# The last gate of a decoder trunk: squares of two token blocks side by side, the last norm's vector on ScalarE, the third block ahead of the fourth, bias rows earlier

## The chip, the cores and the metric

The kernel runs on one core of a Trainium2 chip. The time is the device time of one execution in microseconds, as a median of runs. The core's engines are TensorE (PE: matmuls, PEld: its weight loads), VectorE (DVE), ScalarE (ACT), GpSimd (POOL) and SyncE (SP, which here only issues DMAs). Each engine works its own instruction queue in order, and engines wait for each other by semaphores. DMAs are issued from an engine's queue, here SP's and ScalarE's.

## The reference

A decoder trunk of two layers on 512 tokens of 1024 features, in float32. This is the part that bears on the change: the second layer's gated per-layer embedding and the final norm.

```python
def rmsnorm(x, g):
    xf = x.astype(jnp.float32)
    y = xf * lax.rsqrt(jnp.mean(xf * xf, axis=-1, keepdims=True) + EPS)
    return (y * g.astype(jnp.float32)).astype(x.dtype)

def per_layer_embed(h, p_i, g_norm, w_in, w_gate, b_gate):
    gate = jax.nn.sigmoid(rmsnorm(h, g_norm) @ w_gate + b_gate)
    return (p_i @ w_in) * gate

    for i in range(DEPTH):
        ...
        h = h + conv_ffn(rmsnorm(h, norm_ffn[i]), f_w_up[i], f_conv_w[i], f_conv_b[i], f_w_down[i])
        h = h + per_layer_embed(h, p[i], norm_ple[i], ple_w_in[i], ple_w_gate[i], ple_b_gate[i])
        ...
    return rmsnorm(h, norm_final)
```

## The kernel before

The residual `h` lies with features on the partitions: eight tiles of 128 features x 512 tokens. Every float32 matmul is made of three matmuls on operands that are split into a high and a low part (`mm3`, and `mm3t` where the result has tokens on the partitions; their matmuls have lines L190 to L192 and L201 to L203). Everything up to the last gate runs this way.

The last gate works with tokens on the partitions. There are four token blocks `i` of 128 tokens, and for each the 1024 features in two halves `n` of 512 (for the last block one half and two quarters of 256, see `cuts`). `gate_t(i, n)` issues the matmuls of one such part into a PSUM tile `gt`, 24 of them; the very last part starts with one more matmul, from `rows` (L986), which adds the bias inside the sum. `gated_t(i, n, ps)` issues what follows: `zt`, the scaling by the token's root mean square and the bias (VectorE, L999), the sigmoid `st` (ScalarE, L1004; L996 for the last part, straight from PSUM), the multiply by the embedding `pet` (VectorE, L1005), the add of the residual (VectorE, L1014 for blocks 0 and 1, in place in `hT`; L1021 into `hm` for blocks 2 and 3), and the sum of squares (ScalarE, L1015 and L1023; VectorE, L1028, in the last two parts). For blocks 2 and 3 the result is also multiplied by the last norm's vector `grow` (GpSimd, L1031; VectorE, L1035, into `yt` in the last block).

The residual has to come over to this layout. VectorE transposes it in squares of 32x32 (`turn`, L918: `turned_a` for tokens 0 to 255, `turned_b` for 256 to 511), and `places` (L929) then moves the rows of squares between partitions by DMAs within SBUF into `hT[0]` (blocks 0 and 1) and `hT[1]` (blocks 2 and 3), sixteen DMAs of 64 KB each from SP's queue.

`scaled(i)` makes the final norm's factor of a block: a sum (`fms`, L1040), scale and epsilon (`fin..m`, L360), the power -1/2 on GpSimd (`fin..rt`, L362), for blocks 0 and 1 the multiply by `grow` (VectorE, L1046), then the scaling by the factor (ScalarE, L1047), and for block 2 the DMA to the output. Blocks 0 and 1 are written with features on the partitions: `back()` moves the squares of `hT[0]` back (sixteen DMAs, eight from SP's queue and eight from ScalarE's), transposes them (VectorE, L1057, into `y`) and writes `y` out in four DMAs. `end()` scales the last block by its factor `rfin` (GpSimd, L1063; then ScalarE and VectorE, L1066 and L1068) and writes it.

`bias_rows()` makes the rows that the last part's extra matmul needs. It calls `npl.spread`, which makes `np1d` on VectorE (L342) and then a matmul `np1sp` on TensorE (L346); VectorE's reciprocal (L960) reads that, and a few small casts follow.

The calls stand in the order that is printed at the end of the function. From them a scheduler builds each engine's queue: TensorE's matmuls stay close to the order of the calls, and the other engines' instructions are placed among each other by it. `behind(ins, front)` adds an order of its own: the instruction `ins` stands behind `front` on the same engine. In the kernel before, TensorE's queue has in this stage: the first halves of blocks 0 and 1, the second halves of blocks 0 and 1, the spread `np1sp`, the first halves of blocks 2 and 3, the second half of block 2, and the two quarters of block 3.

Of the kernel before, what the change touches and what calls it, by code (L numbers as in the profile page):

```python
# [8 lines left out]
F32 = mybir.dt.float32  # L9
F32R = mybir.dt.float32r  # L10
AF = mybir.ActivationFunctionType
ALU = mybir.AluOpType

P = 128
D = 1024
S = 512
KD = D // P
# [5 lines left out]
N = S // 2  # L23
# [25 lines left out]
def tile_yoco(ctx: ExitStack, tc: tile.TileContext, t, out: bass.AP, out_b: bass.AP):  # L49
    nc = tc.nc  # L50
# [5 lines left out]
    wp = ctx.enter_context(tc.tile_pool(name="wp", bufs=1))  # L56
# [4 lines left out]
    def psum(name):  # L61
        return mmp.tile([P, S], F32, tag="mm", name=name)
# [60 lines left out]
    def behind(ins, front):  # L123

        tc.add_manual_dep(ins.ins, front.ins.name,
                          mybir.DependencyInfo(mybir.DependencyClass.NoSync, mybir.DependencyReason.DATA),
                          reason="order")
# [80 lines left out]
    def v(name, i):  # L208
        c = VEC[name] + i
        return vec[:, c : c + 1]  # L210

    h = [hp.tile([P, S], F32, tag=f"h{k}", name=f"h{k}") for k in range(KD)]
# [25 lines left out]
    ps = psum("idle").rearrange("p (a b) -> p a b", a=4)  # L238
# [37 lines left out]
    class Norm:  # L276
# [27 lines left out]
        def turn(self):  # L304

            sq = tp.tile([P, S], F32, tag="sq", name=f"{self.name}turn")
            nc.vector.transpose(sq, self.acc)
            self.quarter = const.tile([P, S // 32], F32, tag="quarter", bufs=1, name=f"{self.name}quarter")
            nc.vector.tensor_reduce(self.quarter, sq.rearrange("p (b f) -> p b f", f=32),
                                    axis=mybir.AxisListType.X, op=ALU.add)  # L310
# [265 lines left out]
    for c in range(4):  # L576
# [4 lines left out]
        for j in range(2):  # L581
            m = 2 * c + j
            ps = ups[j]
            z = tp.tile([P, S], F32, tag="hs", name=f"uz{m}")
            nc.vector.tensor_mul(z, ps, rstd)
            u = tp.tile([P, S], F32, tag="sg", name=f"u{m}")
# [20 lines left out]
    turned = const.tile([KD, 2, P], F32, name="turned")  # L607
    ps = psum("turned")
    for i, (name, l) in enumerate((("ple_b_gate", 1), ("norm_final", 0))):
        c0 = VEC[name] + l * KD  # L610
# [97 lines left out]
    box = {}  # L708
# [200 lines left out]
    SQ = 32  # L909
    NQ = P // SQ  # L910

    def squares(pool, tag, name):
        return pool.tile([P, N // SQ, KD, SQ], F32, tag=tag, bufs=1, name=name)

    turned_a = squares(at, "vtl", "turned_a")

    def turn(x, m, c):
        nc.vector.transpose(x[:, :, m, :], h[m][:, c * N : (c + 1) * N].rearrange("p (b t) -> p b t", t=SQ))  # L918

    npl.behind = lambda m: turn(turned_a, m, 0)  # L920
    pet = ffn(1, nf, npl)
# [1 line left out]
    def places(x, y, there):  # L923

        for b in range(NQ):
            for a in range(NQ):
                u = x[SQ * a : SQ * (a + 1), b::NQ].rearrange("p b m d -> p b (m d)")
                w = y[SQ * b : SQ * (b + 1), :, a, :]
                (nc.scalar if a % 2 and not there else nc.sync).dma_start(*((w, u) if there else (u, w)))  # L929


# [8 lines left out]
    parts2 = chunk(S, KD, ahead=2 * WBUFS)  # L940
    r = [f"r{(state['turn'] + j) % 3}" for j in range(3)]
    turned_b = squares(wp, r[0], "turned_b")
    hT = [wp.tile([P, 2, NQ, KD * SQ], F32, tag=r[1 + c], bufs=1, name=f"hT{c}") for c in range(2)]
    places(turned_a, hT[0], True)
    for m in range(KD):
        turn(turned_b, m, 1)
# [3 lines left out]
    brow, grow = (mp.tile([P, D], F32, tag=tag, name=f"row_{tag}") for tag in ("m4", "m5"))  # L950
# [8 lines left out]
    def bias_rows():  # L959
        nc.vector.reciprocal(whole_f[:, 3 * P :], npl.spread(S // 64 - 2, 2))  # L960
        for n, a, at0, lows in ((P, whole_f[:, 3 * P :], 0, 64), (2 * P, brow[:, D - 2 * P :], P, 32)):
            cols = slice(at0, at0 + n)
            nc.scalar.copy(whole[:, cols], a)
            for q in (0, 32, 64):
                if q == lows:
                    nc.vector.tensor_sub(rows[q : q + 1, cols], a[q : q + 1], whole_f[q : q + 1, cols])
                else:
                    nc.scalar.copy(rows[q : q + 1, cols], a[q : q + 1])
# [8 lines left out]
    def by_square(x):  # L977
        return x.rearrange("p (m a d) -> p a m d", a=NQ, d=SQ)

    def gate_t(i, n):  # L980

        c0, w = cuts[i][n]
        ps = psum(f"gt{i}_{n}")[:, :w]
        end = i == LAST and n == len(cuts[i]) - 1
        if end:
            nc.tensor.matmul(ps, rows[:, :P], rows[:, P : 3 * P], start=True, stop=False)  # L986
        mm3t(ps, xs, parts2 if c0 >= S else parts, c0 % S, w, i, first=not end)
        return ps

    def gated_t(i, n, ps):  # L990
        c0, w = cuts[i][n]
        end = i == LAST and n == len(cuts[i]) - 1
        r = rt[:, i : i + 1]
        sg = tp.tile([P, w], F32, tag="sg", name=f"st{i}_{n}")
        if end:
            nc.scalar.activation(sg, ps, AF.Sigmoid, scale=r)  # L996
        else:
            z = tp.tile([P, w], F32, tag="hs", name=f"zt{i}_{n}")
            ins = nc.vector.scalar_tensor_tensor(z, ps, r, brow[:, c0 : c0 + w], op0=ALU.mult, op1=ALU.add)  # L999
            if "y" in box:  # L1000
                behind(ins, box["y"])
            if (i, n) == (LAST, 1):
                behind(ins, box["hm"])
            nc.scalar.activation(sg, z, AF.Sigmoid)  # L1004
        ins = nc.vector.tensor_mul(sg, sg, pet[i][:, c0 : c0 + w])  # L1005
        if end:
            behind(ins, box["yt"])
        turned = hT[i // 2][:, i % 2, :, c0 // NQ : (c0 + w) // NQ]
        sq = tp.tile([P, w], F32, tag="sq", name=f"sqt{i}_{n}")
        if i < 2:  # L1010

            held[i, n] = turned
            split = turned.rearrange("p a (m d) -> p a m d", d=SQ)
            nc.vector.tensor_add(split, split, by_square(sg))  # L1014
            nc.scalar.activation(sq.rearrange("p (a f) -> p a f", a=NQ), turned, AF.Square,  # L1015
                                 accum_out=ssq[:, i, n : n + 1])
            return
        if c0 % S == 0:
            held[i, c0 // S] = tp.tile([P, S], F32, tag=("c0", "acc")[i % 2], name=f"hm{i}_{n}")
        hm = held[i, c0 // S][:, c0 % S : c0 % S + w]  # L1020
        box["hm"] = nc.vector.tensor_add(by_square(hm), turned.rearrange("p a (m d) -> p a m d", d=SQ), by_square(sg))  # L1021
        if i < LAST or n == 0:
            nc.scalar.activation(sq, hm, AF.Square, accum_out=ssq[:, i, n : n + 1])  # L1023
        else:

            if n == 1:
                nc.vector.tensor_scalar(total[:, :1], ssq[:, i, :1], 1.0 / D, EPS, op0=ALU.mult, op1=ALU.add)
            nc.vector.tensor_tensor_reduce(out=sq, in0=hm, in1=hm, scale=1.0 / D, scalar=total[:, n - 1 : n],  # L1028
                                           op0=ALU.mult, op1=ALU.add, accum_out=total[:, n : n + 1])
        if i < LAST:  # L1030
            nc.gpsimd.tensor_mul(hm, hm, grow[:, c0 : c0 + w])  # L1031
        else:
            if not yt:
                yt.append(mp.tile([P, D], F32, tag="m0", name="yt"))
            box["yt"] = nc.vector.tensor_mul(yt[0][:, c0 : c0 + w], hm, grow[:, c0 : c0 + w])  # L1035

    def scaled(i):

        ms = const.tile([P, 1], F32, tag="fms", bufs=2, name=f"fms{i}")
        nc.vector.tensor_reduce(ms, ssq[:, i], axis=mybir.AxisListType.X, op=ALU.add)  # L1040
        r = inv_root(ms, f"fin{i}", 1.0 / D)
        for n in range(2):
            hm = held[i, n]
            if i < 2:
                split = hm.rearrange("p a (m d) -> p a m d", d=SQ)
                nc.vector.tensor_mul(split, split, by_square(grow[:, n * S : (n + 1) * S]))  # L1046
            nc.scalar.activation(hm, hm, AF.Copy, scale=r[:, :1])  # L1047
            if i >= 2:
                nc.sync.dma_start(out_b[i - 2, :, n * S : (n + 1) * S], hm)

    def back():

        x = squares(at, "vtl", "turned_y")
        places(x, hT[0], False)
        y = wp.tile([P, KD, N], F32, tag=r[0], bufs=1, name="y")
        for m in range(KD):
            box["y"] = nc.vector.transpose(y[:, m, :].rearrange("p (b t) -> p b t", t=SQ), x[:, :, m, :])  # L1057
            if m % 2:
                nc.sync.dma_start(out[m - 1 : m + 1].rearrange("k p s -> p k s"), y[:, m - 1 : m + 1, :])

# [9 lines left out]

    for i in range(2):
        gated_t(i, 0, pss[i])
    for i in range(2):
        gated_t(i, 1, gate_t(i, 1))
        scaled(i)
    bias_rows()
    for i in (2, 3):
        gated_t(i, 0, gate_t(i, 0))
    back()
    gated_t(2, 1, gate_t(2, 1))  # L1080
    scaled(2)
    for n in (1, 2):
        gated_t(3, n, gate_t(3, n))
    end()


# [64 lines left out]
```

## Time and profile before

| what | us |
|---|---|
| median of 3 runs (lowest, highest) | 1133.78 (1132.97, 1133.96) |
| the profiled execution's own time | 1134.12 |
| its span, first to last instruction | 1132.4 |
| busy: TensorE, VectorE, ScalarE, GpSimd | 1120.2, 760.1, 513.2, 103.0 |
| mean granted TensorE clock | 0.998 |

A row of the profile in order of time gives the start and the duration in microseconds, the engine, the line of the kernel, the operation, the tile written and the tiles read (buffer numbers left out), the shapes, and how many instructions in a row it stands for; in brackets, the idle time of the engine before it and what ended it. A row of a group gives busy time in all and the mean of one in ns, then the idle time before the group. A row of a DMA tile gives the shortest, median and longest issue in ns. The rows called SPq and ACTq are DMA issues in the queues of SP and ScalarE. The last row of times by window has the window, its length, the busy time of PE, PEld, DVE, ACT and POOL (with instructions), the granted clock, the DMA share and GB/s.

### The profile page before, as it was taken

To read this page: it belongs to the slowest core of one execution; us is meant where nothing else is said; L and a number is where in the kernel's file an instruction comes from. 1 tells how busy PE (TensorE), PEld (TensorE's weight loads), DVE (VectorE), ACT (ScalarE), POOL (GpSimd) and SP (SyncE) were. 2 spreads that over 40 slices of the span, in tenths; PEclk is the share of its full clock that TensorE was granted. 3 is DMA by queue.
4 is the path that set the end of the run, shared out by engine and by line. 5 is a ranking of instruction groups with operands and counts; after the bars stand their busy time and mean duration, and the time that the engine had idled before them with its cause. 6 is when DMAs were issued, how large, how long until landed. Compare 5 with 4: busy or idle time off the path is not lost.

```text
span 1132.4 us, 13327 instructions
## 1 busy us (share of the span) xinstructions
PE 1120.2 (99%) x5118; PEld 930.3 (82%) x5118; DVE 760.1 (67%) x1178; ACT 513.2 (45%) x811; POOL 103.0 (9%) x163
## 2 busy tenths in 40 slices
PE   9999999999999999999999999999999999999996
PEld 7888888888888888888888888888888888888885
DVE  7366477763577457656988997777636773675786
ACT  6533454431334234544656775444313431344543
POOL 2000210000000000012204441000000000000211
PEclk9999999999999999999999999999999999999999
DMA  8322323232222322233134223323222223224333
GB/s 288 135 107 75 112 75 112 78 109 104 83 102 70 109 110 89 98 112 112 49 101 130 75 94 114 130 93 112 77 110 101 77 102 112 90 73 162 109 88 112
DMA packets 29472, 118.55 MB, mean 105 GB/s; under 512 B 3672, under 2 KB 11616, under 8 KB 19936
## 3 DMA queue, kind: packets, MB, share of 16 engines
q1 hardware_dynamic: 28352, 116.71, 30.3%
q10 hardware_dynamic: 1056, 0.98, 0.3%
q8 instruction: 40, 0.66, 0.2%
q14 instruction: 24, 0.20, 0.1%
HBM read 108.24 MB, written 2.11 MB: 97 GB/s over the span
## 4 chain that ended last, share of the span: by engine, by line
PE 92%; DVE 4%; ACT 1%; issue 1%; DMA 1%; POOL 0%; SPq 0%; POOLq 0%; DVEq 0%; ACTq 0%
PE up L190 14%; PE up L192 14%; PE up L191 14%; PE d L192 8%; PE d L190 8%; PE d L191 8%; PE gate L190 1%; PE gate L192 1%; PE u L191 1%; PE u L190 1%; PE u L192 1%; PE gate L191 1%; PE o L191 1%; PE o L192 1%; PE o L190 1%
## 5 line engine op out<-in xcount | busy, mean ns | idle before, releaser
L163 ACT CAST wh<-wraw 128x1024 fp32r<-128x1024 f32 (+2 forms) x197 | 202.1, 1028 | 265.0 <-PE d L191 131.3
L164 DVE TENSOR_TENSOR wl<-wraw,wh 128x1024 fp32r<-128x1024 f32 (+1 forms) x198 | 238.5, 1206 | 122.2 <-ACT wh L163 121.6
L190 PE MATMUL up<-nf00h,wh 128*128 128x512 f32 x352 | 137.1, 390 | 0.0
L190 PE MATMUL up<-nf10h,wh 128*128 128x512 f32 x352 | 137.0, 389 | 0.0
L192 PE MATMUL up<-nf00h,wl 128*128 128x512 f32 x352 | 137.0, 389 | 0.0
L192 PE MATMUL up<-nf10h,wl 128*128 128x512 f32 x352 | 137.0, 389 | 0.0
L191 PE MATMUL up<-nf10l,wh 128*128 128x512 f32 x352 | 137.0, 389 | 0.0
L191 PE MATMUL up<-nf00l,wh 128*128 128x512 f32 x352 | 137.0, 389 | 0.0
L190 PE MATMUL d<-ah,wh 128*128 128x512 f32 x352 | 136.9, 389 | 0.0
L191 PE MATMUL d<-al,wh 128*128 128x512 f32 x352 | 136.9, 389 | 0.0
L192 PE MATMUL d<-ah,wl 128*128 128x512 f32 x352 | 136.9, 389 | 0.0
L403 ACT ACTIVATE c<-hs,vec 128x512 f32<-128x512 f32 x88 | 71.5, 815 | 72.8 <-DVE hs L399 72.1
L404 DVE SCALAR_TENSOR_TENSOR c<-hs,vec,c 128x511 f32<-128x511 f32 x88 | 65.8, 748 | 34.2 <-ACT c L403 34.2
L379 DVE TENSOR_TENSOR h<-h,d 128x512 f32<-128x512 f32 x56 | 38.4, 686 | 72.7 <-PE d L192 72.7
L192 PEld LDWEIGHTS up<-nf10h,wl 128*128 128x128 f32 x352 | 66.1, 188 | 13.8
L191 PEld LDWEIGHTS up<-nf00l,wh 128*128 128x128 f32 x352 | 66.1, 188 | 13.8
L192 PEld LDWEIGHTS d<-ah,wl 128*128 128x128 f32 x352 | 66.1, 188 | 13.7
L191 PEld LDWEIGHTS d<-al,wh 128*128 128x128 f32 x352 | 66.1, 188 | 13.7
L190 PEld LDWEIGHTS up<-nf10h,wh 128*128 128x128 f32 x352 | 66.1, 188 | 13.7
L190 PEld LDWEIGHTS d<-ah,wh 128*128 128x128 f32 x352 | 66.1, 188 | 13.7
L192 PEld LDWEIGHTS up<-nf00h,wl 128*128 128x128 f32 x352 | 66.1, 188 | 13.7
L190 PEld LDWEIGHTS up<-nf00h,wh 128*128 128x128 f32 x352 | 66.1, 188 | 13.6
(406 smaller groups left out, 1953.4 us busy)
## 6 DMA issues: line engine op xcount, KB each, us to landing
wraw<-in_w_up SPq DMA_DIRECT2D x44, 1024.0 KB, 4.7
wraw<-in_w_down SPq DMA_DIRECT2D x16, 896.0 KB, 4.5
wraw<-in_w_down SPq DMA_DIRECT2D x8, 1024.0 KB, 4.8
wraw<-in_w_gate SPq DMA_DIRECT2D x8, 1024.0 KB, 4.8
wraw<-in_w_u SPq DMA_DIRECT2D x4, 1024.0 KB, 5.5
wraw<-in_w_out SPq DMA_DIRECT2D x4, 1024.0 KB, 4.7
wraw<-in_w_q SPq DMA_DIRECT2D x4, 1024.0 KB, 4.8
wraw<-in_w_o SPq DMA_DIRECT2D x4, 1024.0 KB, 4.9
```

The source lines that it names most:

```text
L163: nc.scalar.copy(hi, src)
L164: nc.vector.tensor_sub(low, src, hi.bitcast(F32))
L190: nc.tensor.matmul(ps, wh[:, a:b], xh, start=st, stop=False)
L191: nc.tensor.matmul(ps, wh[:, a:b], xl, start=False, stop=False)
L192: nc.tensor.matmul(ps, wl[:, a:b], xh, start=False, stop=en)
L379: nc.vector.tensor_add(h[m], h[m], ps)
L403: nc.scalar.activation(c, hs, AF.Identity, bias=v("conv_b", l * 2 * NJ + col), scale=cw[2])
L404: nc.vector.scalar_tensor_tensor(c[:, 1:], hs[:, : S - 1], cw[1], c[:, 1:], op0=ALU.mult, op1=ALU.add)
```

## The change

It has four parts. In `squares` and `hT`, the squares of the two token blocks of a tile now stand beside each other, so that a DMA of `places` has one run of 512 elements on each of its 32 partitions where it had two of 256; the transposes write and read in that order (`in_order`). The multiply of blocks 0 and 1 by `grow` on VectorE (L1046) goes; in its place ScalarE multiplies the transposed `y` by the vector `norm_final`, eight instructions of 128x256 behind the transposes of `back()`. The third block's two halves both stand ahead of `back()` and of the fourth block, and block 2's scaling stands behind the last sigmoid. And `bias_rows()` is called ahead of the second halves of blocks 0 and 1.

```diff
+    def in_order(x, m):
+
+        return x.rearrange("p (b i) m d -> p m i b d", i=2)[:, m]
+
     def turn(x, m, c):
-        nc.vector.transpose(x[:, :, m, :], h[m][:, c * N : (c + 1) * N].rearrange("p (b t) -> p b t", t=SQ))
+        nc.vector.transpose(in_order(x, m), h[m][:, c * N : (c + 1) * N].rearrange("p (i b t) -> p i b t", i=2, t=SQ))
...
-                u = x[SQ * a : SQ * (a + 1), b::NQ].rearrange("p b m d -> p b (m d)")
-                w = y[SQ * b : SQ * (b + 1), :, a, :]
+                u = x[SQ * a : SQ * (a + 1), 2 * b : 2 * b + 2].rearrange("p i m d -> p (i m d)")
+                w = y[SQ * b : SQ * (b + 1), a].rearrange("p i f -> p (i f)")
...
-    hT = [wp.tile([P, 2, NQ, KD * SQ], F32, tag=r[1 + c], bufs=1, name=f"hT{c}") for c in range(2)]
+    hT = [wp.tile([P, NQ, 2, KD * SQ], F32, tag=r[1 + c], bufs=1, name=f"hT{c}") for c in range(2)]
...
         if end:
-            nc.scalar.activation(sg, ps, AF.Sigmoid, scale=r)
+            box["sg"] = nc.scalar.activation(sg, ps, AF.Sigmoid, scale=r)
...
-        turned = hT[i // 2][:, i % 2, :, c0 // NQ : (c0 + w) // NQ]
+        turned = hT[i // 2][:, :, i % 2, c0 // NQ : (c0 + w) // NQ]
...
             hm = held[i, n]
-            if i < 2:
-                split = hm.rearrange("p a (m d) -> p a m d", d=SQ)
-                nc.vector.tensor_mul(split, split, by_square(grow[:, n * S : (n + 1) * S]))
-            nc.scalar.activation(hm, hm, AF.Copy, scale=r[:, :1])
+            ins = nc.scalar.activation(hm, hm, AF.Copy, scale=r[:, :1])
+            if i == 2:
+                behind(ins, box["sg"])
...
-            box["y"] = nc.vector.transpose(y[:, m, :].rearrange("p (b t) -> p b t", t=SQ), x[:, :, m, :])
+            box["y"] = nc.vector.transpose(y[:, m, :].rearrange("p (i b t) -> p i b t", i=2, t=SQ), in_order(x, m))
+            nc.scalar.activation(y[:, m, :], y[:, m, :], AF.Copy, scale=v("norm_final", m))
...
     for i in range(2):
         gated_t(i, 0, pss[i])
+    bias_rows()
     for i in range(2):
         gated_t(i, 1, gate_t(i, 1))
         scaled(i)
-    bias_rows()
-    for i in (2, 3):
-        gated_t(i, 0, gate_t(i, 0))
+    for n in range(2):
+        gated_t(2, n, gate_t(2, n))
     back()
-    gated_t(2, 1, gate_t(2, 1))
+    for n in range(3):
+        gated_t(3, n, gate_t(3, n))
     scaled(2)
-    for n in (1, 2):
-        gated_t(3, n, gate_t(3, n))
     end()
```

In the changed program's queues, TensorE has the spread `np1sp` between the first and the second halves of blocks 0 and 1. VectorE's order up to `np1d` is unchanged: the last transposes of `turned_b`, the two `zt` of the first halves, `np1d`, and only then the multiplies. Its transposes of `back()` stand behind the third block's `fin2m` and ahead of the fourth block's first `zt`. ScalarE has, from block 1's scaling on: two DMA issues of the way back, the third block's first sigmoid, two issues, its square, three issues, its second sigmoid, one issue, its square, the eight scalings of `y`, and then the fourth block's sigmoids.

## The prediction

> **What bounds the kernel now.** I read the busy shares first, then the waits of TensorE, then the last 50 us of each engine in order of time. The first two:
>
> ```profile
> PE 1120.2 (99%) x5118; PEld 930.3 (82%) x5118; DVE 760.1 (67%) x1178; ACT 513.2 (45%) x811; POOL 103.0 (9%) x163
> PE v L203 <- DVE wl L164: 1.2, 2, 0.7
> PE idle L240 <- DVE minus_half L243: 1.1, 1, 1.1
> ```
>
> TensorE is busy for 99% of the span, and its longest single wait in the whole kernel is 1.1 us, at the start. So the span is the stream of matmuls plus what follows the last of them. Any microsecond in which TensorE's queue stands still in the middle is a microsecond at the end, unless what follows the stream gets shorter. What follows it, from the views in order of time:
>
> ```profile
> 1123.25 0.28 PE L203 MATMUL gt<-own_al,np10h 128*128 128x256 f32 x1
> 1116.88 2.73 DVE L1057 STREAM_TRANSPOSE y<-turned_y 128x256 f32<-128x256 f32 x8 [0.22 <-issue]
> 1119.54 0.71 DVE L999 SCALAR_TENSOR_TENSOR zt<-gt,np1rows,row_m 128x512 f32<-128x512 f32 x1
> 1122.28 0.48 DVE L999 SCALAR_TENSOR_TENSOR zt<-gt,np1rows,row_m 128x256 f32<-128x256 f32 x1
> 1123.27 1.26 POOL L1031 TENSOR_TENSOR hm<-hm,row_m 128x512 f32<-128x512 f32 x1 [10.14 <-ACT sqt L1023]
> 1123.48 0.15 DVE L360 TENSOR_SCALAR fin2m<-fms 128x1 f32<-128x1 f32 x1
> 1123.55 1.26 DVE L1005 TENSOR_TENSOR st<-st,pet 128x256 f32<-128x256 f32 x1
> 1123.57 0.47 ACT L996 ACTIVATE st<-gt,np1rows 128x256 f32<-128x256 f32 x1
> 1124.85 0.42 DVE L1021 TENSOR_TENSOR hm<-hT,st 128x256 f32<-128x256 f32 x1
> 1126.06 0.42 DVE L1005 TENSOR_TENSOR st<-st,pet 128x256 f32<-128x256 f32 x1
> 1126.51 0.42 DVE L1021 TENSOR_TENSOR hm<-hT,st 128x256 f32<-128x256 f32 x1
> 1126.97 0.48 DVE L1028 CUSTOM_DVE_ANT_0 sqt<-hm,total 128x256 f32<-128x256 f32 x1
> 1127.54 0.66 POOL L1063 TENSOR_TENSOR rfin<-total,minus_half 128x1 f32<-128x1 f32 x1 [2.33 <-DVE total L1028]
> 1128.23 0.68 DVE L1066 TENSOR_SCALAR yt<-yt,rfin 128x256 f32<-128x256 f32 x2 [0.43 <-POOL rfin L1063]
> ```
>
> The last matmul ends at 1123.25 + 0.28 = 1123.53 and ScalarE has its sigmoid at 1124.04, but VectorE multiplies that result only at 1126.06. VectorE is 2.0 us behind TensorE here, for two reasons: the eight transposes of the way back and the third block's second half go ahead of the fourth block's, and one multiply of 128x256 takes 1.26 us where its twin takes 0.42, while GpSimd runs its own multiply (1123.27 to 1124.53). From the last matmul to the final scaling at 1128.23 it is 4.70 us, and from there to the end of the span 4.17.
>
> **The change part by part. First, the bias rows sooner.** This edit moves one matmul, the spread `np1sp` (L346), in TensorE's program order: from behind both blocks' second halves to ahead of them. It reads `np1d`, made by VectorE (L342).
>
> ```profile
> 1089.95 0.39 PE L203 MATMUL gt<-wl,np10h 128*128 128x512 f32 x1
> 1090.17 0.39 PE L201 MATMUL gt<-own_ah,np10h 128*128 128x512 f32 x1
> 1095.61 0.39 PE L201 MATMUL gt<-own_ah,np10h 128*128 128x512 f32 x1
> 1101.05 0.22 PE L346 MATMUL np1sp<-np1d,ones 128*128 128x128 f32 x1
> 1101.11 0.45 PE L201 MATMUL gt<-wh,np10h 128*128 128x512 f32 x1
> 1091.41 1.10 DVE L918 STREAM_TRANSPOSE turned_b<-h 128x256 f32<-128x256 f32 x3
> 1092.54 1.41 DVE L999 SCALAR_TENSOR_TENSOR zt<-gt,np1rows,row_m 128x512 f32<-128x512 f32 x2
> 1093.87 0.28 DVE L342 TENSOR_TENSOR np1d<-pick,np1hl 128x128 fp32r<-128x128 f32 x1
> ```
>
> Before, `np1d` is done at 1093.87 + 0.28 = 1094.15 and wanted at 1101.05: 6.9 us to spare. In the changed program VectorE's order up to `np1d` is the same (the last transposes of `turned_b`, two `zt`, then `np1d`), but the spread now stands where the 1090.17 matmul stood. TensorE waits from there to 1094.15, hands over in about 0.1, and the spread's own 0.06 (1101.05 to 1101.11) is paid in both kernels: 3.98 + 0.1 = 4.1 us of standing still. The 169 matmuls of the gate that follow (five halves of 24, a quarter of 24, a quarter of 25) are queued behind it, and nothing covers the loss: every one of them is 4.1 us later, the last ending at 1127.6. What the rows were moved for, the bias matmul at the head of the last part, does not wait before (TensorE's waits, above, hold none in this part), so there is nothing to win.
>
> That stall depends on the matmuls keeping their order. The Trainium skill (TensorE: Matmul & The Clock Gate, "Step-by-step: what each phase is for") says that only weight loads are pulled ahead and matmuls stay in program order. The one long wait that the trace has, at the start, cannot show either.
>
> **Second, the order of the blocks.** A block half is 1095.61 - 1090.17 = 5.44 us of matmuls. With the stream restarted at 1094.3, halves end (last issue plus 0.16) at 1105.3 for block 1, 1116.2 for the third block's second half, 1121.7 for the fourth's first, 1124.6 and 1127.6 for its two quarters. What VectorE does then needs these rows:
>
> ```profile
> L1005 DVE TENSOR_TENSOR st<-st,pet 128x512 f32<-128x512 f32 x7 | 4.7, 681 | 3.9 <-ACT st L1004 3.9
> L1004 ACT ACTIVATE st<-zt 128x512 f32<-128x512 f32 x7 | 4.4, 628 | 15.4 <-DVE zt L999 13.5 <-DMA turned_y<-hT 1.9
> L1021 DVE TENSOR_TENSOR hm<-hT,st 128x512 f32<-128x512 f32 x3 | 2.1, 693 | 0.1
> L1004 ACT ACTIVATE st<-zt 128x256 f32<-128x256 f32 x1 | 0.4, 401 | 0.0
> L1046 DVE TENSOR_TENSOR hT<-hT,row_m 128x512 f32<-128x512 f32 x4 | 2.7, 686 | 0.2 <-ACT sqt L1015 0.2
> ```
>
> VectorE's queue holds the transposes behind `fin2m` of the third block. Before, that chain (zt, sigmoid, multiply, add, square, two small ones) takes from 1119.54 to 1123.48 + 0.15, so 4.09. After, it starts at 1116.3, and the transposes at 1120.35. They take 2.66 up to the next instruction (1116.88 to 1119.54), so the fourth block's `zt` comes at 1123.0, though its matmuls were done at 1121.7. Behind it: zt 0.71 to 1123.7, sigmoid, multiply, add.
>
> **Third, the last norm's vector on ScalarE.** Four multiplies of 0.686 (2.7 us) leave VectorE, at a place where it had gaps, so they are worth nothing there; but they also shorten the chain to the way back. Eight scalings of 128x256 come to ScalarE, ahead of the fourth block's sigmoid. The trace has no such copy of that size. From below it is the 0.40 of a sigmoid of this shape, from above the 0.47 of one that reads PSUM and a scale (1123.57). I take 0.47, with 0.07 overlapped 0.40 from start to start: from the first transpose's end at 1120.75 eight end at 1124.0. The sigmoid wanted at 1123.75 is held 0.25 by them, since ScalarE works its queue in order. At 0.33 apart the hold is gone; at 0.47 it is 0.8.
>
> Now the sum: sigmoid 1124.0 to 1124.65, multiply 0.68 and add 0.69 with their handovers to 1126.1. The quarter's zt (0.41 to the next instruction), yt 0.62, total 0.1 and multiply 0.45 stand ahead of its add: 1126.05 + 1.58 = 1127.6. From that add to the end of the last square sum, before takes 1124.85 to 1126.97 + 0.48, so 2.60; after ends at 1130.2 against 1127.45: **2.75 later**. GpSimd's multiply starts after the third block's second square, near 1120.0, and with its 1.26 ends near 1121.2, beside the transposes, so the stall of 1.26 - 0.42 = 0.84 is gone. The floor is where VectorE has caught up: last matmul 1127.6, sigmoid 0.47, multiply 0.42, add 0.42, square 0.48 and handovers, 1129.6, which is 2.1 later. So the new order wins between 1.3 and 2.0 us of the tail, against 4.1 lost.
>
> **Fourth, the squares side by side.** Each transfer of the 48 keeps its bytes and moves one run of 512 elements in place of two of 256; each transpose writes in another order.
>
> ```profile
> L651 SPq DMA_DIRECT2D kh<-kh x4: 531/566/596, 580.0 to 583.1; - x4
> L929 SPq DMA_DIRECT2D hT<-turned_b x16: 586/595/602, 1092.6 to 1102.2; - x16
> 1107.10 0.56 POOL L362 TENSOR_TENSOR fin1rt<-fin1m,minus_half 128x1 f32<-128x1 f32 x1 [3.75 <-DVE fin1m L360]
> 1107.69 1.34 ACT L1047 ACTIVATE hT<-hT,fin1rt 128x512 f32<-128x512 f32 x2 [1.52 <-POOL fin1rt L362]
> turned_y<-hT ACTq DMA_DIRECT2D x8, 64.0 KB, 2.0
> 1109.06 1.54 ACTq L929 DMA_DIRECT2D turned_y<-hT  x2
> 1111.68 1.91 ACTq L929 DMA_DIRECT2D turned_y<-hT  x3
> ```
>
> An issue costs 0.595 now; the nearest row with one run, 64x512, has 0.566, and the first ones on ScalarE 0.77. I take 0.6, between. The loads of `hT` (the last issued at 1102.2) are there long before the third block's add reads them, near 1114. The way back starts after block 1's chain: 1105.4 + 4.1 + 0.56 + 1.34 and handovers, 1111.5. On ScalarE stand two issues, a sigmoid, two, a square, three (1115.2 to 1117.1), then the third block's second sigmoid, wanted at 1117.05: no hold. The last issue ends at 1117.8 and lands 2.0 later, at 1119.8, 0.5 ahead of the transposes that read it. Cheaper issues win nothing; at 0.77 each the sigmoid is held 0.5 and so is all behind it. A transpose in the new order: below as now, above 0.1 more (no reason for a gain); four lie in TensorE's wait, so up to 0.4.
>
> **Rivals.** *The clock falls in the gap.* TensorE would be idle from 1090.34 to 1094.2, 3.9 us. These rows show the clock going down 4.4 us after the last matmul's end (within the 0.1 us from 1127.90, whose mean is 0.73), and what a slow clock costs:
>
> ```profile
> 1127.90:1128.00 0.10, 0.00 (x0) 0.00 (x0) 0.00 (x0) 0.00 (x0) 0.10 (x1) 0.73 0.97 369
> 1.12 4.10 PE L240 MATMUL idle<-idle 128*128 128x512 f32 x9 [1.12 <-DVE minus_half L243]
> 5.06 0.63 PE L507 MATMUL v<-wh,n00h 128*128 128x512 f32 x2
> ```
>
> Nine matmuls start 0.46 apart ((4.10 - 0.39) / 8), and 3.9 us after the first of them they start 0.24 apart. A restart from the slow clock would cost half of about 3.5 us, 1.7, on top: 2.7 + 1.7 = 4.4, so 1138.2. For it: the gap is nearly as long as the one that did it. Against: it is 0.5 shorter. The Trainium skill (TensorE: Matmul & The Clock Gate, "HAM oscillation — how this bites in real kernels") warns of idle gaps above 3.4 us, watched in windows that run on their own. By that rule alone a gap of 3.9 holds a whole idle window in (3.9 - 3.4) / 3.4, some 15% of executions, as an estimate from that page.
>
> *TensorE does not stand still* (the matmuls behind the spread start at 1090.2 as before): then 2.7 - 4.1 = -1.4, so 1132.4, not slower. It decides if the first matmul on `own_ah` starts before 1093. Against it: every wait in the trace holds its whole queue.
>
> *VectorE comes to `np1d` sooner.* Between the end of its input `np1hl` and 1093.87 lie three transposes and two `zt`, 1.10 + 1.41; without them the wait is 1.6 and the sum 2.7 - 2.5 = +0.2. A wait of 1.4 is the point of balance. Against it: they stand ahead of it in the program.
>
> **How the numbers follow.** The profiled execution took 1134.12 (span 1132.4), 0.34 above the median of 1133.78; I add the 2.7 to both, 1136.8 and **1136.5**. Chances: this case 60%, clock 25%, no stall 6%, shorter stall 9%. Within 0.2% (2.3 us, about what can be told from no change) the likeliest case sits near the edge: its own range is +2.1 to +3.5, and I give a quarter of it to "same". Slower: 45 of it and 24 of the clock's 25, 69; same: 15, 1, 4 of the 6 and 8 of the 9, 28; faster 3. The range 1134.8 to 1138.6 leaves out the case without a stall, half of the shorter one and the top of the slow clock.
>
> **What would show it.** A TensorE wait on `np1d` of about 4 us at the spread; last matmul near 1127.6; granted clock 1.00 just after the wait, or else 0.5; `zt` of the fourth block right behind the transposes; no 128x256 multiply above 0.5 us; from the last matmul to the final scaling 2.7 to 3.4 in place of 4.70. I am wrong if the wait is under 2 us, if the transposes wait for the way back, or if ScalarE holds the last sigmoid.

## The result, and the profile after

| | before | after |
|---|---|---|
| median of 6 runs each (lowest, highest), us | 1133.71 (1132.97, 1133.96) | 1139.58 (1139.44, 1140.66) |
| the profiled execution's own time, us | 1134.12 | 1139.59 |
| its span, us | 1132.4 | 1137.9 |
| mean granted TensorE clock | 0.998 | 0.996 |

The changed kernel takes 1.0053 of the time before, interval 1.0043 to 1.0063: 5.87 us slower. The forecast was slower by 2.75, at 1136.5, with a range up to 1138.6. The direction came, at more than twice the size.

The waits of TensorE in the kernel after (line waited for: us in total, times, longest):

```profile
PE np1sp L346 <- DVE np1d L342: 3.9, 1, 3.9
PE idle L240 <- DVE minus_half L243: 1.1, 1, 1.1
...
```

The predicted wait is there, and nothing like it was there before. TensorE in order of time around it, in the kernel after:

```profile
1089.32 0.39 PE L203 MATMUL gt<-wl,np10h 128*128 128x512 f32 x1
1093.58 0.33 PE L346 MATMUL np1sp<-np1d,ones 128*128 128x128 f32 x1 [3.87 <-DVE np1d L342]
1093.74 0.44 PE L201 MATMUL gt<-own_ah,np10h 128*128 128x512 f32 x1
1094.02 0.39 PE L202 MATMUL gt<-own_ah,np10l 128*128 128x512 f32 x1
...
1094.56 0.63 PE L201 MATMUL gt<-own_ah,np10h 128*128 128x512 f32 x1
1094.98 0.63 PE L202 MATMUL gt<-own_ah,np10l 128*128 128x512 f32 x1
...
1098.13 0.39 PE L201 MATMUL gt<-own_ah,np10h 128*128 128x512 f32 x1
...
1100.85 0.39 PE L201 MATMUL gt<-own_ah,np10h 128*128 128x512 f32 x1
```

TensorE ends its last matmul of block 1's first half at 1089.71 and starts the spread at 1093.58. The matmuls behind it go at 0.23 to 0.28 from start to start at first, then at 0.42, then at 0.23 again. Times by window of the same kernel (window, length, busy PE, PEld, DVE, ACT, POOL, then the granted clock, DMA share and GB/s) show why:

```profile
1093.00:1094.00 1.00, 0.42 (x2) 0.41 (x3) 0.58 (x3) 0.96 (x2) 0.00 (x0) 1.00 0.51 123
1094.00:1095.00 1.00, 1.00 (x5) 0.73 (x4) 1.00 (x2) 0.07 (x1) 0.00 (x0) 0.69 0.30 74
1095.00:1096.00 1.00, 1.00 (x4) 0.81 (x3) 1.00 (x2) 0.73 (x3) 0.00 (x0) 0.50 0.53 131
1097.00:1098.00 1.00, 1.00 (x4) 0.77 (x4) 0.68 (x2) 0.84 (x3) 0.00 (x0) 0.60 0.46 111
1098.00:1099.00 1.00, 1.00 (x6) 0.83 (x5) 0.00 (x0) 0.50 (x2) 0.00 (x0) 1.00 0.47 115
```

The clock is still full when the matmuls resume at 1093.74, and is halved 0.64 us later: a mean of 0.69 in the window from 1094 means 0.62 us at half, so it fell at 1094.38; by 0.60 in the window from 1097 it rose at 1097.80. The half behind the spread (24 matmuls) runs from 1093.74 to 1100.85, 7.11 us, where a half took 5.44: 1.67 us are lost.

The end of the kernel after, in order of time:

```profile
1117.37 0.75 DVE L1003 SCALAR_TENSOR_TENSOR zt<-gt,np1rows,row_m 128x512 f32<-128x512 f32 x1 [1.26 <-PE gt L203]
1117.42 1.97 ACTq L933 DMA_DIRECT2D turned_y<-hT  x3
1119.43 0.63 ACT L1008 ACTIVATE st<-zt 128x512 f32<-128x512 f32 x1 [2.11 <-DMA turned_y<-hT]
1122.34 1.30 POOL L1035 TENSOR_TENSOR hm<-hm,row_m 128x512 f32<-128x512 f32 x1 [3.65 <-ACT sqt L1027]
1122.96 2.73 DVE L1060 STREAM_TRANSPOSE y<-turned_y 128x256 f32<-128x256 f32 x8 [0.25 <-issue]
1123.44 3.31 ACT L1061 ACTIVATE y<-y,vec 128x256 f32<-128x256 f32 x8 [1.17 <-DVE y L1060]
1125.62 0.71 DVE L1003 SCALAR_TENSOR_TENSOR zt<-gt,np1rows,row_m 128x512 f32<-128x512 f32 x1
1126.65 0.61 ACT L1008 ACTIVATE st<-zt 128x512 f32<-128x512 f32 x1
1128.35 0.28 PE L203 MATMUL gt<-own_al,np10h 128*128 128x256 f32 x1
1131.54 0.42 DVE L1009 TENSOR_TENSOR st<-st,pet 128x256 f32<-128x256 f32 x1
1133.72 0.68 DVE L1070 TENSOR_SCALAR yt<-yt,rfin 128x256 f32<-128x256 f32 x2 [0.44 <-POOL rfin L1067]
```

From the last matmul's end (1128.35 + 0.28 = 1128.63) to the final scaling (1133.72) it is 5.09 us, longer than the 4.70 before, where the prediction had about 3.35. The third block's second `zt` is done at 1118.12, and its sigmoid starts only at 1119.43: ScalarE's queue still held issues of the way back. The prediction had written "no hold" there.

All later readings use one measure. Before `np1d` nothing is changed in TensorE's order, and its end wanders between executions (1094.15 in the profile before, 1093.52 after). From it I count to the last matmul's end (called the stream below), and from there to the final scaling (the tail); from the final scaling to the end of the execution nothing differs by more than 0.04.

| profiled execution | `np1d` to last matmul (stream) | to the final scaling (tail) | sum |
|---|---|---|---|
| before | 29.38 | 4.70 | 34.08 |
| after | 35.11 | 5.09 | 40.20 |

So in these two executions the change costs 6.12 us behind `np1d` (5.87 by the medians): 5.73 in the stream, of which 1.67 is the slow clock and the remaining 4.06 the standing still, and 0.39 in the tail.

### The profile page after: what moved, and what is told of

The parts are those of the page before. It is cut to its first block, busy times and chain, and to the rows that moved or that the text cites. A ratio compares the mean times of both kernels' runs of the same rounds, so it can differ in the third digit from the quotient of the medians.

```text
span 1137.9 us, 13330 instructions
## 1 busy us (share of the span) xinstructions
PE 1121.9 (99%) x5118; PEld 931.8 (82%) x5118; DVE 756.5 (66%) x1174; ACT 515.9 (45%) x819; POOL 102.5 (9%) x163
## 4 chain that ended last, share of the span: by engine, by line
PE 92%; DVE 3%; issue 2%; ACT 1%; DMA 1%; POOL 1%; SPq 0%; POOLq 0%; ACTq 0%; DVEq 0%
PE up L190 14%; PE up L192 14%; PE up L191 14%; PE d L191 8%; PE d L192 8%; PE d L190 8%; PE q L190 1%; PE q L192 1%; PE gate L190 1%; PE q L191 1%; PE gate L192 1%; PE u L192 1%; PE gate L191 1%; PE u L190 1%; PE u L191 1%
## 5 line engine op out<-in xcount | busy, mean ns | idle before, releaser
L191 PEld LDWEIGHTS up<-nf10l,wh 128*128 128x128 f32 x352 | 66.1, 188 | 13.8
```

The costliest lines, as they stand in the source:

```text
L191: nc.tensor.matmul(ps, wh[:, a:b], xl, start=False, stop=False)
```

## The experiments

### The bias rows, taken back and made alone

```diff
 r1_rows_late: the changed kernel
-    bias_rows()
     for i in range(2):
         gated_t(i, 1, gate_t(i, 1))
         scaled(i)
+    bias_rows()
 r2_rows_early_alone: the kernel before
+    bias_rows()
     for i in range(2):
         gated_t(i, 1, gate_t(i, 1))
         scaled(i)
-    bias_rows()
```

> The changed kernel with the bias rows called where they stood before the change, all else kept. Theory (the wait at the spread and the slow clock behind it are the whole loss): TensorE has no wait of 3.9 us, the granted clock stays 1.00 to the last matmul, the last matmul ends 5.8 us sooner than in the changed kernel, near 1122.9 by its clock, and the time is 1133.8. Rival (the new order of the blocks itself loses too, since ScalarE's DMA issues hold the third block): the time stays 0.3 to 1 above the 1133.7 of before, 1134.0 to 1134.7. Rival (the new order gains the 1.4 that the prediction gave it): 1132.3.

> The kernel before with the bias rows alone moved ahead, none of the other three edits. Theory: a wait of 3.9 us at the spread, then about 3.4 us at half clock, the last matmul 5.8 us later, and nothing taken off by the end that follows: 1133.7 + 5.8 = 1139.5. Rival (the wait is partly taken up by VectorE, which is 2 us behind TensorE at the end of the kernel before): 1137.5.

Without the earlier rows the changed kernel took 1134.23, ratio 1.0003 (0.9994 to 1.0012). With them alone the kernel before took 1139.73, ratio 1.0052 (1.0039 to 1.0066). The stream took 29.38 in the first and 35.15 in the second. So this one call is the whole stall, and the slow clock with it. The first one's time lies in the range of the rival of its expectation, that ScalarE's issues hold the third block, and its tail of 5.58, with three of the four parts still in, was longer than before; an instruction fetch, told of next, lay in its way back.

### The stall filled

```diff
 r3_filled: the changed kernel
+    ps = psum("filled")
+    for k in range(15):
+        nc.tensor.matmul(ps, xs[0][0][:, :P], parts[0][0][:, :S], start=k == 0, stop=k == 14)
     bias_rows()
```

The 15 matmuls fill 3.56 us of the wait; nothing reads what they make.

> The changed kernel with 15 more matmuls of 128x512 ahead of the spread, whose result nothing reads; they take 15 x 0.227 = 3.4 us, inside the wait of 3.9, and the spread still starts when its operand is there. Theory (the clock falls because TensorE stands idle): granted clock 1.00 throughout, the first block half behind the spread takes 5.44 us again in place of 7.11, and the time is 1139.6 - 1.7 = 1137.9. Rival (the slow matmuls behind the spread have another cause): 1139.6.

It took 1136.64, ratio 1.0025 (1.0016 to 1.0034). The clock stayed up and the stream took 33.54, that is 29.38 + 4.16: the standing still alone. That was expected, but the time fell by 2.94, where 1.7 was expected from the clock (the stream got 1.57 shorter). The rest is in the tail, in order of time in this run:

```profile
1115.97 0.75 DVE L1003 SCALAR_TENSOR_TENSOR zt<-gt,np1rows,row_m 128x512 f32<-128x512 f32 x1 [1.25 <-PE gt L203]
1116.75 0.63 ACT L1008 ACTIVATE st<-zt 128x512 f32<-128x512 f32 x1 [1.28 <-DVE zt L1003]
1119.89 0.15 DVE L360 TENSOR_SCALAR fin2m<-fms 128x1 f32<-128x1 f32 x1
1120.29 2.73 DVE L1060 STREAM_TRANSPOSE y<-turned_y 128x256 f32<-128x256 f32 x8 [0.24 <-issue]
1122.94 0.71 DVE L1003 SCALAR_TENSOR_TENSOR zt<-gt,np1rows,row_m 128x512 f32<-128x512 f32 x1
1126.94 0.28 PE L203 MATMUL gt<-own_al,np10h 128*128 128x256 f32 x1
1131.05 0.68 DVE L1070 TENSOR_SCALAR yt<-yt,rfin 128x256 f32<-128x256 f32 x2 [0.44 <-POOL rfin L1067]
```

Here the sigmoid starts 0.03 after its `zt`, and the tail is 1131.05 - 1127.22 = 3.83, 1.26 less than in the changed kernel. The two kernels' DMAs of the way back differ; first the changed kernel's (shortest, median and longest issue in ns), then this run's:

```profile
L933 ACTq DMA_DIRECT2D turned_y<-hT x8: 515/603/1880, 1112.5 to 1119.5; - x8
L933 SPq DMA_DIRECT2D turned_y<-hT x8: 507/590/2163, 1112.6 to 1118.5; - x8
DMA to landing us min/median/max: 1.9/2.2/4.2
```

```profile
L933 ACTq DMA_DIRECT2D turned_y<-hT x8: 514/602/815, 1111.1 to 1116.8; - x8
L933 SPq DMA_DIRECT2D turned_y<-hT x8: 507/590/694, 1111.2 to 1115.5; - x8
DMA to landing us min/median/max: 1.9/2.0/2.2
```

In the changed kernel one issue on each queue took about 2 us in place of 0.6. In the same stretch the trace has one packet of the queue that fetches instructions (queue 8; over the whole execution 40 packets and 0.66 MB, so 16 KB each). It began at 1114.43 and took 1.75; the DMA view from 1114.43 to 1116.2, in part:

```profile
q8 instruction: 1, 0.02, 6.2%
issues: line engine op xcount, KB each, median us to landing
turned_y<-hT ACTq DMA_DIRECT2D x2, 64.0 KB, 3.6
turned_y<-hT SPq DMA_DIRECT2D x1, 64.0 KB, 3.6
```

The transfers issued in this window landed after 3.6 us in place of 2.0. In the filled kernel this fetch began at 1109.08, ahead of the first issue.

### Which of the two it is: short matmuls in the same number

The same 15 matmuls on 64 columns each move the fetch as far, if it goes by the number of TensorE's instructions, but leave a gap of 2.27.

```diff
 r5_tiny_filled: the changed kernel
+        nc.tensor.matmul(ps[:, :64], xs[0][0][:, :P], parts[0][0][:, :64], start=k == 0, stop=k == 14)
```

> The changed kernel with 15 more matmuls, now of only 64 columns, ahead of the spread (their result is read by nothing). They leave TensorE nearly idle in the wait, but move TensorE's instruction count by the same 30 instructions as the 15 long ones did, and so the place where its next block of instructions is fetched (in the changed kernel this transfer falls into the way back, at 1114.4, and two DMA issues take 1.9 and 2.2 us there). Theory (two separate costs: 1.67 of slow clock, and about 1.3 of ScalarE held by DMA issues while the instruction fetch is in their way): the clock still falls, no DMA issue is above 0.9 us, 1139.6 - 1.3 = 1138.3. Rival (the long DMA issues come from the slow clock or from the order): they stay, 1139.6. Rival (weight loads alone keep the clock up): 1136.6.

It took 1138.72, ratio 1.0043 (1.0028 to 1.0058). The clock still fell (the stream took 35.14), the fetch began at 1110.99, ahead of the way back, no issue was longer than 0.81, and the tail was 3.82. So the two costs come apart: this run pays the clock and not the fetch, at 1.27 less in the trace and 0.86 less in the medians than the changed kernel.

### How long a gap the clock bears

```diff
 r9_fill8 and r10_fill11: as r3_filled
-    for k in range(15):
+    for k in range(8):
+    for k in range(11):
```

> The changed kernel with 8 more matmuls of 128x512 ahead of the spread (nothing reads them): TensorE's idle time in the wait falls from 3.87 to about 2.05, while the spread starts when it did. Seen so far: the clock fell at the end of windows of 3.41 us in which TensorE was busy for 23% and 35%, and not at one with 71%. Here a window holds at least 1 - 2.05 / 3.41 = 40%. Theory (a window counts as idle while it is busy for less than about half): the clock falls in those executions whose windows lie so that one holds nearly all of the idle time, so the times fall into two groups, near 1136.7 and near 1138.3. Rival (it needs a window that is idle but for a third or less): all near 1136.7. Rival (any gap of 2 us does it): all near 1138.3.

> The same with 11 more matmuls: idle time 1.37 us, every window at least 60% busy. Theory: the clock stays, all executions near 1136.7. Rival (any gap does it): up to 1138.3.

With 8 it took 1138.46, ratio 1.0039 (1.0025 to 1.0053); with 11 it took 1136.85, ratio 1.0027 (1.0016 to 1.0037). TensorE with 8, in order of time:

```profile
1090.11 1.98 PE L1079 MATMUL filled<-wh,np10h 128*128 128x512 f32 x8
1094.13 0.33 PE L346 MATMUL np1sp<-np1d,ones 128*128 128x128 f32 x1 [2.05 <-DVE np1d L342]
```

The gap is from 1092.09 to 1094.13, 2.04 us. Times by window of that run:

```profile
1094.00:1095.00 1.00, 0.87 (x4) 0.79 (x5) 0.58 (x2) 0.55 (x1) 0.00 (x0) 0.97 0.35 84
1095.00:1096.00 1.00, 1.00 (x4) 0.71 (x4) 1.00 (x3) 0.50 (x3) 0.00 (x0) 0.50 0.47 115
```

By the mean of 0.97 the clock fell at 1094.94. In each of the four traces with a fall inside the stream (the changed kernel, r2, r5 and r9) the low stretch is 3.41 us long (1094.38 to 1097.80 above), and from that fall to the one after the last matmul it is eleven times as long, so I read it as windows of 3.41 us at whose end the clock is set. One more window can be read in r7_vector_alone, a run of the section after next: its last matmul, and the window in which its clock falls:

```profile
1122.47 0.28 PE L203 MATMUL gt<-own_al,np10h 128*128 128x256 f32 x1
1127.00:1128.00 1.00, 0.00 (x0) 0.00 (x0) 0.64 (x2) 0.29 (x1) 0.00 (x0) 0.97 0.82 307
```

The matmuls end at 1122.75 and the clock falls at 1127.94, so the window before that fall ended at 1124.53 and did not take the clock. The share of such a window in which TensorE worked:

| window that ends at | work in it | clock after it |
|---|---|---|
| 1094.38 in the changed kernel | from 1093.58: 0.80, 23% | half |
| 1095.14 in r5_tiny_filled | from 1093.93: 1.21, 35% | half |
| 1094.94 in r9_fill8 | 0.57 and 0.81, 40% | half |
| 1124.53 in r7_vector_alone | to 1122.75: 1.63, 48% | full |
| 1094.16 in r11_spread_first (below) | from 1092.00: 2.16, 63% | full |
| 1124.53 in the kernel before | to 1123.53: 2.41, 71% | full |

The window ends of the last three are counted back from a later fall (1127.94, 1128.29, 1127.95). So 40% lost the clock and 48% kept it. A gap of 1.38, with 11 fillers, cannot take a window below about 60% and did nothing; the changed kernel's 3.87 takes some window to 43% or less wherever it falls, which lies between the two. All six of its executions fit a fall: none lies below 1139.4, where one without the fall would be near 1137.9. The five executions with 8 fillers, at 1137.77 to 1138.87, show no two clear groups. The lowest of them has a mean granted clock of 0.998, and the traced executions show 0.996 or 0.997 with such a fall and 0.997 or 0.998 without; so it seems to have kept the clock, and whether every gap of 2.04 us loses it is not shown.

### The rows one block later

```diff
 r4_rows_between: the changed kernel
-    bias_rows()
     for i in range(2):
         gated_t(i, 1, gate_t(i, 1))
         scaled(i)
+        if i == 0:
+            bias_rows()
```

> The changed kernel with the bias rows called between the second halves of blocks 0 and 1, so that the spread stands 5.4 us later in TensorE's queue and its operand has been there for over 1 us. Theory (it is the wait that costs, not the rows' being earlier): no wait, full clock, the same time as with the rows late, 1133.8. Rival (VectorE's reciprocal and ScalarE's casts among the blocks cost something of their own): 0.3 to 1 above that.

It took 1133.59, ratio 0.9997 (0.9988 to 1.0007): one half of matmuls (5.44) ahead of the spread covers the whole wait. The stream took 29.39 and the tail 4.59. So where nothing stands still, the three other parts win 0.11 us of the tail, not the 0.87 of the filled kernel. Its rows in order of time say where the rest is:

```profile
1111.50 0.75 DVE L1003 SCALAR_TENSOR_TENSOR zt<-gt,np1rows,row_m 128x512 f32<-128x512 f32 x1 [0.34 <-PE gt L203]
1111.75 1.24 ACTq L933 DMA_DIRECT2D turned_y<-hT  x2
1113.04 0.63 ACT L1008 ACTIVATE st<-zt 128x512 f32<-128x512 f32 x1 [1.13 <-DVE zt L1003]
```

The third block's second `zt` is done at 1112.25 and its sigmoid waits for two ordinary issues, 0.62 each, until 1113.04. In the stalled kernels the way back had a head start on the matmuls (4.84 us from its first issue to that `zt` in the filled kernel, 3.08 here); without the stall the hold of 0.8 is there even with no fetch in the way.

### The other parts alone

```diff
 r6_layout_alone: the kernel before, with the hunks of squares, places, hT and the transposes
+                u = x[SQ * a : SQ * (a + 1), 2 * b : 2 * b + 2].rearrange("p i m d -> p (i m d)")
+                w = y[SQ * b : SQ * (b + 1), a].rearrange("p i f -> p (i f)")
...
 r7_vector_alone: the kernel before
-                nc.vector.tensor_mul(split, split, by_square(grow[:, n * S : (n + 1) * S]))
...
+            nc.scalar.activation(y[:, m, :], y[:, m, :], AF.Copy, scale=v("norm_final", m))
 r8_order_alone: the kernel before; block 2's scaling stands behind the last sigmoid on ScalarE
...
-    for i in (2, 3):
-        gated_t(i, 0, gate_t(i, 0))
+    for n in range(2):
+        gated_t(2, n, gate_t(2, n))
     back()
-    gated_t(2, 1, gate_t(2, 1))
-    scaled(2)
-    for n in (1, 2):
+    for n in range(3):
         gated_t(3, n, gate_t(3, n))
+    scaled(2)
```

> The kernel before with the squares side by side alone. Theory (an issue costs about 0.6 with one run or two, and the transposes the same 0.4): the same time within 0.3, 1133.9. Rival (shorter issues free ScalarE): 1133.3.

> The kernel before with the last norm's vector on ScalarE alone. VectorE loses four multiplies of 0.69 where it had gaps; ScalarE gets eight scalings of 0.41 in a stretch where it was idle for 3.8 us; the way back starts about 1.3 earlier. Without the added order, the third block's two scalings come to stand ahead of the last sigmoid on ScalarE. Theory: the same within 0.4, 1133.9; if those two scalings hold the last sigmoid, up to 1.3 more, 1135.2. Rival (VectorE's load matters): 1133.0.

> The kernel before with the third block ahead of the fourth (and its scaling behind the last sigmoid) alone. Theory (the multiply stalled by GpSimd, 0.84, goes, but the transposes now stand ahead of the fourth block's first half and ScalarE is held by DMA issues): 1133.4 to 1134.2. Rival (the prediction's gain of 1.4 belongs to the order): 1132.5.

The layout alone took 1133.7, ratio 0.9998 (0.9989 to 1.0008): nothing. The order alone took 1133.49, ratio 0.9996 (0.9986 to 1.0006), with a tail of 4.37: 0.3 at most, and not clear of no change. The vector alone took 1135.69, ratio 1.0016 (1.0007 to 1.0026), slower by 1.8, 0.5 above the higher of its expected times, with a tail of 6.76. Two rows of it in order of time:

```profile
1125.60 1.33 ACT L1044 ACTIVATE hm<-hm,fin2rt 128x512 f32<-128x512 f32 x2 [1.75 <-POOL fin2rt L362]
1127.33 0.43 DVE L1005 TENSOR_TENSOR st<-st,pet 128x256 f32<-128x256 f32 x1 [0.83 <-ACT st L996]
```

Without the order that goes with it, ScalarE scales block 2 ahead of the last sigmoid, and VectorE waits 0.83 for that. The fourth block's first sigmoid is 0.28 later behind the eight scalings (VectorE waits 0.98 there, 0.70 before). The remaining 0.9 is there already at the fourth block's first `zt`: in this execution a fetch began 0.7 after the way back, and issues took up to 1.60. In this run and in r1 it is the vector's part that brings the two together: without VectorE's multiplies the way back starts 13.99 us behind `np1d` in both, and 14.91 behind it in the kernel before, while the fetch comes 14.5 to 14.7 behind it in all three.

### The spread's input made sooner

```diff
 r11_spread_first: the changed kernel; the spread is made behind the last mm3t, ahead of the last two
 transposes of turned_b and of both zt
+    tail = npl.spread(S // 64 - 2, 2)
-        nc.vector.reciprocal(whole_f[:, 3 * P :], npl.spread(S // 64 - 2, 2))
+        nc.vector.reciprocal(whole_f[:, 3 * P :], tail)
```

> The changed kernel with the spread's operand made ahead of the last two transposes and the two zt on VectorE, right behind the values that it needs; TensorE's order is kept. The wait falls from 3.87 to about 1.8 us. Theory: the last matmul is 2.0 later than in the kernel before, in place of 5.7; what follows it takes 3.8 in place of 4.7 unless the instruction fetch falls into the way back; so 1133.8 + 2.0 - 0.9 = 1134.9, and 1136.5 where the clock falls. Rival (the wait is not what costs): 1139.6.

It took 1136.02, ratio 1.0022 (1.0013 to 1.0032), so it missed its expectation. TensorE waited 1.75 (the spread started at 1092.00) and the clock stayed up in the profiled execution, both as expected. But a fetch began 1.6 after the way back, an issue took 1.64, and the tail was 4.54, 0.71 above the undisturbed one. Four of its ten executions, at 1136.72 to 1137.54, are some 0.6 to 1.9 slower than the other six. Three of them have a mean granted clock of 0.996, as executions with a fall have (and four of r7_vector_alone, which has no gap), and the one at 1136.72 has 0.998; and a gap of 1.75 leaves every window at least 49% of work, a share that kept the clock in the table above. The four were not traced, and what slowed them stays open.

### A version without the loss

```diff
 r12_transposes_between: r8_order_alone, with the transposes called behind the fourth block's first half,
 and free to mix with it
-    back()
-    for n in range(3):
+    xy = back()
+    gated_t(3, 0, gate_t(3, 0))
+    turned_back(*xy, 0, KD)
+    for n in (1, 2):
         gated_t(3, n, gate_t(3, n))
...
-            if "y" in box:
-                behind(ins, box["y"])
```

> The kernel before with the third block ahead of the fourth (as in the run with that order alone), and with the transposes of the way back called behind the fourth block's first half: on VectorE they then stand one by one between its zt, multiply and add, where VectorE waits for the sigmoid. The squares, the last norm's vector and the bias rows stay as before the change. Theory (after the third block VectorE is what the end waits for, and its idle time is what can be won): 0.7 less than with the order alone, 1132.8, below both kernels. Rival (the fourth block's first half has time enough): 1133.5.

It took 1132.77 against 1133.89 of the kernel before in the same runs, ratio 0.999 (0.9981 to 0.9999): 1.1 us ahead of the kernel before, just clear of no change, and 6.8 ahead of the changed kernel. VectorE in order of time:

```profile
1117.57 0.45 DVE L1061 STREAM_TRANSPOSE y<-turned_y 128x256 f32<-128x256 f32 x1 [0.25 <-issue]
1117.94 0.71 DVE L999 SCALAR_TENSOR_TENSOR zt<-gt,np1rows,row_m 128x512 f32<-128x512 f32 x1
1118.57 1.08 DVE L1061 STREAM_TRANSPOSE y<-turned_y 128x256 f32<-128x256 f32 x3
1119.58 0.65 DVE L1003 TENSOR_TENSOR st<-st,pet 128x512 f32<-128x512 f32 x1
```

The transposes run while ScalarE makes the sigmoid and the square, where VectorE used to wait for it. The tail is 3.80, the stream 29.38. Of the change only the order of the blocks is in this version; the place of the transposes is new.

## Why the prediction was right in direction and short in size

From `np1d` on, in us, the undisturbed tail taken from the filled kernel:

| term | predicted | measured |
|---|---|---|
| TensorE stands still at the spread | 4.1 | 4.06 |
| the clock falls in the gap | 0 (as a rival, 1.7 at 25%) | 1.67 |
| the tail, undisturbed | 3.35 - 4.70 = -1.35 | 3.83 - 4.70 = -0.87 |
| issues of the way back hold ScalarE | 0 | 5.09 - 3.83 = 1.26 |
| sum | 2.75 | 6.12 |

**The standing still** was right within 0.1: 4.06 is what is left of the stream's 5.73 beside the slow clock, and the filled kernel, with the clock up, has 4.16. Moving that call by itself (the kernel before with early rows) brings all of it, and the rest of the change moves none of the stream. That matmuls do not pass one that waits is shown too: nothing ran between 1089.71 and 1093.58, in agreement with the rule of the Trainium skill that the prediction named.

**The clock** was the step that failed first. It was priced well (1.7, measured 1.67) and ruled wrongly. The prediction read the one fall that it had, 4.4 us after the last matmul, as a gap that is needed, and found 3.9 to be 0.5 short. But that fall came a whole window late, since the window in which the work ended was still 71% busy. By the table above what counts is the share of one window: 40% and less lost the clock, 48% and more kept it, and a gap of 3.87 takes some window to 43% or less wherever it lies. The Trainium skill (TensorE: Matmul & The Clock Gate, "HAM oscillation — how this bites in real kernels") warns of gaps above 3.4 us; this case's traces show the fall after gaps of 2.04 and 2.27 as well, so the measurement decides for the shorter one. The 15% worked out from that rule was the same mistake: it asked for a window with no work at all. The rows for a better bound were in the prediction, the last matmul's end and the fall; the step not taken was to ask what a window of 3.4 would have held there. The answer, 71%, leaves open any share below it, so it would have spoken for a higher chance, not for certainty.

**ScalarE's issues** were the second step that failed. "No hold" rested on 0.6 for each of eight issues, which is what an undisturbed issue takes (medians of 0.590 and 0.603 after). What was not reckoned with is an instruction fetch among them. The Trainium skill (Perfetto Trace Analysis, "DMA Instruction — HWDGE (DVE, Sync)") says, for issues from VectorE and SyncE, that the recorded time of an issue contains a wait for a lock on the block that makes the descriptors, and not the data's movement. The 2.16 on SP's queue and the 1.88 on ScalarE's, in place of 0.6 for the same 64 KB, fit a wait within the issue; which lock or which earlier landing it waits for, no run here shows. That the fetch goes with it is seen across all fourteen profiled kernels. The start of the fetch against the first issue of the way back:

| fetch starts | profiled executions (r1 to r12 by the first part of their names) | longest issue, us |
|---|---|---|
| 0.2 to 2.0 before it | before, r3, r4, r5, r6, r8, r9, r10 | 0.80 to 0.84 |
| 0.3 after it | r12 | 0.98 |
| 0.7 to 1.9 after it | after, r1, r2, r7, r11 | 1.60 to 2.16 |

In r5 the fetch was moved and the stall and the slow clock kept, by more instructions on TensorE far from the DMAs, and the long issues went. It is still a coincidence of two events that could both follow from something third; no run here took the fetch itself away.

**The tail** was 0.48 too hopeful. A quarter of a microsecond is the pause ahead of the transposes (0.24 in the filled kernel), whose like stood in the prediction's own row of before, 0.22. Most of the rest is 0.05 on the third block's `zt` and 0.12 from the fourth block's `zt` to the last square. The other steps held: the eight scalings ran 0.41 apart (3.31 in all) where 0.40 was taken, the sigmoid behind them was held 0.3 (1126.33 to 1126.65) where 0.25 was, the transposes took 2.66 as before, GpSimd's multiply lies beside them (1122.34) and no 128x256 multiply is above 0.5.

**Vector and layout** cost next to nothing once the order goes with them and no fetch falls in: r4, with all three, took 1133.59, the order alone 1133.49. The prediction did not say that the vector is slow by itself: 1.8, of which the order takes away the 0.83 of block 2's scaling, nor that it brings the way back ahead of the fetch, as in r1 and r7.

Two rivals fell. TensorE did stand still, and VectorE did not come to `np1d` sooner; made to come sooner, it left a wait of 1.75, near the 1.6 that the prediction gave for it, but the kernel stayed 2.1 slower than before.

## What to carry to other kernels

A matmul moved up in TensorE's queue is worth what its input's readiness allows, and costs the whole queue when it waits: find the row that makes the input, and move the call only as far as work of that length still stands ahead of it (here one half of 5.44 us was enough). Price a hole in a matmul stream by its length plus one slow window, 1.67 us here, which a hole of some 2 us can already bring; 11 matmuls put into the hole bought the clock back here. An engine that both computes and issues DMAs is held by an issue for as long as the issue takes, and that took 1.88 us in place of 0.6 where an instruction fetch fell among the issues.

## What was not expected of the hardware

The clock went to half after a window in which TensorE had worked 40% of the time, in a gap of 2.04 us, and stayed down for 3.41 us. One packet of 16 KB, an instruction fetch, went with single issues of 64 KB transfers that took up to 2.16 us in place of 0.6 and landings after 3.6 in place of 2.0. It seems to be TensorE's fetch: in all fourteen traces it starts when TensorE has started 5030 to 5034 matmuls, counted in the trace, though the time of that runs from 1107.98 to 1114.43 us, and 15 more matmuls ahead of it moved it from 1114.43 to 1110.99 or earlier. So two kernels that differ in a few instructions far away can differ by about a microsecond at the end (here 1.27 in the traces, 0.86 in the medians).
